# Weight splits of a two-block network move from GpSimd to VectorE, and five modulation blocks into the input projection

## The chip, the cores and the metric

The kernel runs on one core of one Trainium2 chip. The metric is the device time of one execution in microseconds. The engines of the core are named TensorE (PE in the rows), VectorE (DVE), ScalarE (ACT), GpSimd (POOL) and SyncE (SP), which issues most of the transfers. Each of them works through its own instructions in the order in which they were written or scheduled.

## The reference, cut to what matters

Two blocks run one after the other on 256 tokens of width 1024, all in float32. The first has two layers, each with a mixer and a routed network over 16384 experts; the vectors that modulate it come from one small product of the condition with `ada_w`, in twelve blocks of 512 columns per layer. The second has two layers of gated network, hybrid mixer, gated network.

```python
sh1, sc1, g1, sh2, sc2, g2 = jnp.split(cond @ ada_w[layer] + ada_b[layer], 6, axis=-1)
h = modulate(rmsnorm(x, norm1_g[layer]), sh1, sc1)
...
    y, yc = even_mixer(h, hc, ...)   # layer 0: p = h @ w_in, short convolution, gated delta rule,
                                     # neighbourhood attention, output projection
    y, yc = odd_mixer(h, hc, ...)    # layer 1: latent attention
x = x + g1[:, None, :] * y
x = x + g2[:, None, :] * peer_ffn(modulate(rmsnorm(x, norm2_g[layer]), sh2, sc2), ...)

# second block, for each of its two layers
h = swiglu(rms_norm(x, ffn1_pre[l]), ffn1_w_gate_up[l], ffn1_w_down[l])
x = x + 0.5 * rms_norm(h, ffn1_post[l])
h = hybrid_mixer(rms_norm(x, mix_pre[l]), w_in[l], ...)
x = x + rms_norm(h, mix_post[l])
h = swiglu(rms_norm(x, ffn2_pre[l]), ffn2_w_gate_up[l], ffn2_w_down[l])
x = x + 0.5 * rms_norm(h, ffn2_post[l])
```

## The kernel before

**Products in three passes.** Nearly all large products run on TensorE as three matmuls (`mm3`, L311 to L314): high part by high part, high by low, low by high. A weight slab is loaded raw by `load` (L330, 1 MB, on SyncE's queue). `hl_part` (L338) then makes the two parts of a piece of 128x1024: ScalarE casts the high part (`wh`, L343), and another engine subtracts it from the raw weight to get the low part (`wl`, written through the helper `tt`, L317). This subtraction is called a split below. The argument `e` of `hl_part` names its engine, and VectorE is the default. `feed` (L354) hands out pieces with a lookahead of two; `Slab` (L375) makes all pieces of a slab at once. In `Slab`, `e="half"` and `late=True` both give the first piece to GpSimd.

**Where GpSimd splits.** There are 84 of them: 12 for the six weight slabs of the convolution (`w_gd`, in `even_mixer`); 20 in the first layer's route stage (two at its start, the other 18 in the generator `ahead`, which makes expert weights in advance) and 22 in the second layer's (four at its start, 18 in `ahead`); and 30 at the entries of the second block's networks and mixers: five at each of four gated networks (`up_tokens`: two slabs of two pieces and the first piece of a third slab) and five at each of two hybrid mixers.

**The stages, with their times in the profiled execution.** 56 to 232 us is the input projection of the first layer in `even_mixer`: a loop of twelve convolution tiles (to about 150 us), each with one `tensor_scalar` and four `scalar_tensor_tensor` of 128x512 on VectorE; eight tiles for the attention; and the products for v and z. From 232 to 520 us, the attention stage (phase `A2`) runs several generators in turn: the inverses and the chain of the gated delta rule, the neighbourhood attention, and `ada_thread`. From 640 to 960 and from 2060 to 2300 us are the route stages: `router` picks the experts (a chain of small maximum searches on VectorE), `gbuild` builds masks out of fp16 products of 128x1024 on VectorE, and `u_ahead` runs the pieces of `ahead` through TensorE. From 2870 us on is the second block, with entries (called borders) near 2891, 3085, 3305, 3503, 3702 and 3923 us.

**The modulation blocks.** `ada_thread` (L468) makes a block of 512 columns as a sum over k: a memset of the accumulator on GpSimd, eight slices of the weight, and for each two `scalar_tensor_tensor` of 128x512 on VectorE (L326); behind that a few small matmuls. Blocks 4 to 9 of the first layer run so in the attention stage; blocks 0 to 3 are made earlier, on TensorE.

**A border of the second block.** `edge_rows` (L1942) squares the tiles of the finished product on ScalarE, takes `newton` (L405; a reciprocal root in eleven one-element steps on VectorE) of the sums, adds the scaled tile to the row store (L326, 128x512), and transposes the new rows on TensorE (L436). It does so for the two halves of 128 tokens in turn, with a second `newton` for the norm ahead of the next product. `Rows.finish` spreads the norms over a tile by one small matmul (L309). `up_tokens` and `pairs_by_token` start the next product while this goes on.

## Time and profile before

| what | value |
|---|---|
| median of 3 runs | 4130.0 us (4127.25 to 4146.29) |
| time of the profiled execution | 4132.58 us |
| its span, first to last instruction | 4130.8 us |
| TensorE busy | 3926.5 us (95%), mean granted clock 0.979 |
| VectorE busy | 2971.3 us (72%) |
| ScalarE busy | 1912.1 us (46%) |
| GpSimd busy | 752.8 us (18%) |
| moved by DMA | 862.66 MB, mean 209 GB/s |

The busy time of an engine is a mean over all stages. The granted clock is a share of full speed, and a matmul's end is modelled, so a busy TensorE is not one at its peak.

### The profile page before, as it was taken

To read this page: it belongs to the slowest core of one execution; us is meant where nothing else is said; L and a number is where in the kernel's file an instruction comes from. 1 tells how busy PE (TensorE), PEld (TensorE's weight loads), DVE (VectorE), ACT (ScalarE), POOL (GpSimd) and SP (SyncE) were. 2 spreads that over 40 slices of the span, in tenths; PEclk is the share of its full clock that TensorE was granted. 3 is DMA by queue.
4 is the path that set the end of the run, shared out by engine and by line. 5 is a ranking of instruction groups with operands and counts; after the bars stand their busy time and mean duration, and the time that the engine had idled before them with its cause. 6 is when DMAs were issued, how large, how long until landed. Compare 5 with 4: busy or idle time off the path is not lost.

```text
span 4130.8 us, 63830 instructions
## 1 busy us (share of the span) xinstructions
PE 3926.5 (95%) x24927; PEld 3537.2 (86%) x24927; DVE 2971.3 (72%) x5618; ACT 1912.1 (46%) x3241; POOL 752.8 (18%) x579
## 2 busy tenths in 40 slices
PE   8999999997999999999989999999999999999999
PEld 5877878897888787888789988888989988989988
DVE  4468579986998988847599555656668765668765
ACT  3334344772333332335558544544445454545454
POOL 2133302113444555400132000000000000000000
PEclk9999999999999999999999999999999999999999
DMA  4222133668999999843247866665454545444543
GB/s 170 92 85 79 36 148 112 221 257 309 357 362 367 369 373 362 329 173 114 87 159 279 296 227 228 229 225 202 178 187 174 184 173 180 178 179 174 184 173 143
DMA packets 234974, 862.66 MB, mean 209 GB/s; under 512 B 18944, under 2 KB 116096, under 8 KB 164528
## 3 DMA queue, kind: packets, MB, share of 16 engines
q1 hardware_dynamic: 197808, 724.35, 48.9%
q0 software_dynamic: 36864, 134.23, 8.5%
q8 instruction: 195, 3.19, 0.3%
q14 instruction: 107, 0.88, 0.1%
HBM read 795.97 MB, written 62.55 MB: 208 GB/s over the span
## 4 chain that ended last, share of the span: by engine, by line
PE 56%; DVE 15%; DMA 5%; issue 4%; POOL 2%; ACT 1%; SPq 0%; DVEq 0%; POOLq 0%; ACTq 0%
PE p L312 18%; PE p L314 18%; PE p L313 18%; DVE t L317 5%; DVE t L326 3%; DMA t<-in_pvr,c 3%; DVE wl L317 2%; POOL t L1443 2%; PE p L309 2%; DMA w<-in_pv 1%; PE p L436 1%; DVE t L1448 1%; DMA t<-in_pur,c 0%; DVE t L321 0%; ACT wh L343 0%
## 5 line engine op out<-in xcount | busy, mean ns | idle before, releaser
L317 DVE TENSOR_TENSOR wl<-w,wh 128x1024 fp32r<-128x1024 f32 (+1 forms) x933 | 1131.2, 1218 | 695.6 <-ACT wh L343 673.1
L343 ACT CAST wh<-w 128x1024 fp32r<-128x1024 f32 x1017 | 1058.8, 1048 | 986.9 <-PE p L314 435.7
L312 PE MATMUL p<-t,wh 128*128 128x256 f32 (+2 forms) x4784 | 1456.6, 305 | 20.0 <-ACT wh L343 5.3
L314 PE MATMUL p<-t,wl 128*128 128x256 f32 (+2 forms) x4784 | 1442.3, 302 | 5.3 <-DVE wl L317 3.3
L313 PE MATMUL p<-t,wh 128*128 128x256 f32 (+2 forms) x4784 | 1439.6, 301 | 1.4 <-DVE t L317 1.4
L312 PEld LDWEIGHTS p<-t,wh 128*128 128x128 f32 x4784 | 912.3, 191 | 40.8 <-ACT wh L343 7.2
L314 PEld LDWEIGHTS p<-t,wl 128*128 128x128 f32 x4784 | 912.3, 191 | 19.0 <-DVE wl L317 4.8
L313 PEld LDWEIGHTS p<-t,wh 128*128 128x128 f32 x4784 | 912.8, 191 | 17.0 <-DVE t L317 1.7
L312 PE MATMUL p<-wh,t 128*128 128x512 f32 (+3 forms) x2134 | 816.4, 383 | 27.0 <-ACT t L402 12.7
L313 PE MATMUL p<-wl,t 128*128 128x512 f32 (+3 forms) x2134 | 815.9, 382 | 22.0 <-DVE wl L317 20.8
L314 PE MATMUL p<-wh,t 128*128 128x512 f32 (+3 forms) x2134 | 813.4, 382 | 6.6 <-DVE t L317 4.6
L317 POOL TENSOR_TENSOR wl<-w,wh 128x1024 fp32r<-128x1024 f32 x84 | 225.4, 2693 | 1967.7 <-ACT wh L343 1697.7
L312 PEld LDWEIGHTS p<-wh,t 128*128 128x128 f32 x2134 | 408.3, 191 | 105.0 <-ACT t L402 14.8
L313 PEld LDWEIGHTS p<-wl,t 128*128 128x128 f32 x2134 | 408.3, 191 | 97.2 <-DVE wl L317 27.1
L314 PEld LDWEIGHTS p<-wh,t 128*128 128x128 f32 x2134 | 406.5, 191 | 87.3 <-DVE t L317 8.7
L317 DVE TENSOR_TENSOR t<-t,t 128x256 f32<-128x256 f32 (+10 forms) x732 | 352.3, 486 | 64.0 <-ACT t L402 41.5
L326 DVE SCALAR_TENSOR_TENSOR t<-t,c,t 128x512 f32<-128x512 f32 (+2 forms) x367 | 327.7, 918 | 39.6 <-DMA t<-in_pvr,c 21.1
L402 ACT CAST t<-t 128x256 fp32r<-128x256 f32 (+3 forms) x314 | 138.7, 446 | 353.3 <-DVE t L317 353.3
L309 PE MATMUL p<-t,t 128*128 128x128 f32 (+3 forms) x1536 | 225.8, 301 | 2.2 <-DVE t L326 1.9
L1443 POOL DMA_INDIRECT t<-in_pvr,c x128 | 197.5, 1543 | 155.7 <-DVE t L326 127.5
L1443 POOL DMA_INDIRECT t<-in_pur,c x128 | 171.9, 1343 | 240.5 <-DVE c L1448 198.9
L309 PEld LDWEIGHTS p<-t,t 128*128 128x128 f32 (+1 forms) x1536 | 192.9, 192 | 25.5 <-issue 11.3
(200 smaller groups left out, 3000.2 us busy)
## 6 DMA issues: line engine op xcount, KB each, us to landing
w<-in_pu SPq DMA_DIRECT2D x128, 1024.0 KB
w<-in_pv SPq DMA_DIRECT2D x128, 1024.0 KB
w<-in_fgu SPq DMA_DIRECT2D x88, 1024.0 KB
w<-in_hin SPq DMA_DIRECT2D x48, 1024.0 KB
w<-in_fdn SPq DMA_DIRECT2D x44, 1024.0 KB
gd<-t SPq DMA_DIRECT2D x20, 2048.0 KB
t<-in_ada_w SPq DMA_DIRECT2D x56, 512.0 KB
t<-gd SPq DMA_DIRECT2D x32, 768.0 KB
```

Source lines behind the costliest of these rows:

```text
L309: nc.tensor.matmul(o, l, r, start=first, stop=last)
L312: nc.tensor.matmul(o, l[0], r[0], start=first, stop=False)
L313: nc.tensor.matmul(o, l[0], r[1], start=False, stop=False)
L314: nc.tensor.matmul(o, l[1], r[0], start=False, stop=last)
L317: return (e or nc.vector).tensor_tensor(o, a, b, op)
L326: nc.vector.scalar_tensor_tensor(o, a, s, b, op0=op0, op1=op1)
L343: i = nc.scalar.copy(hi[:, :m], raw[:, s : s + m])
L402: nc.scalar.copy(dst[0], src)
L436: nc.tensor.transpose(o, i, ident[:n, :n])
L1443: nc.gpsimd.indirect_dma_start(r, None, src, at)
L1448: nc.vector.tensor_tensor_reduce(r, r, xr, 1.0, 0.0, ALU.mult, ALU.add, act[:, s : s + 1])
```

## The change

The `e` arguments that name GpSimd are taken away at the route stages' starts, in `ahead`, and at the entries of the second block, and so is the rule for first pieces in `Slab`: these 72 splits run on VectorE, and the 12 of `w_gd` stay on GpSimd. Of the six modulation blocks of the attention stage, five (4 to 8) are made in the input projection: a step of the generator `ad` behind each of the last four convolution tiles, each attention tile, and every second tile of v and z. Their weights come in 512 KB tiles (`AW`, two buffers) and two accumulators take turns. Block 9 stays behind. The scheduler may place the instructions elsewhere than the source has them.

```diff
--- before.py
+++ after.py
@@ -377,7 +377,7 @@
             raw = load(src, n)
             self.gran = gran
             self.parts = [
-                hl_part(raw, s, min(gran, n - s), nc.gpsimd if s == 0 and (late or e == "half") else None if e == "half" else e, late)
+                hl_part(raw, s, min(gran, n - s), e, late)
                 for s in range(0, n, gran)
             ]
 
@@ -684,6 +684,15 @@
         kn = vk = None
         qk = T("T16", [P, 8, 512])
         gz = pdr.tile([P, 4, 512], F32, tag="gz", name="gz")
+
+        def raws(l, n):
+            for q in range(4):
+                w = T("AW", [P, 1024])
+                nc.sync.dma_start(w, A["ada_w"][l, 2 * n + q // 2, :, q % 2 * 1024 : (q % 2 + 1) * 1024])
+                for k in range(2):
+                    yield w[:, k * 512 : (k + 1) * 512]
+
+        ad = ada_thread([(0, n, 0) for n in range(4, 9)], "AD", "G2", raws)
         with W1():
             srcs = [(A["w_gr"], 1024, None)]
             srcs += [(A["w_gd"][s], 2048, nc.gpsimd) for s in range(6)]
@@ -754,12 +763,15 @@
                 if j > 0:
                     for _ in range(3):
                         next(gstep, None)
+                if j > 7:
+                    next(ad, None)
             knT = T("T8", [P, 4, 512])
             for j in range(8):
                 W = get()
                 ps = PS("ab"[j % 2])
                 stat_tile(ps, W, 0, hT)
                 flush()
+                next(ad, None)
                 if j < 4:
                     nc.scalar.activation(qk[:, j, :], ps, AF.Copy, scale=0.125)
                 else:
@@ -791,6 +803,8 @@
                     for t in range(4):
                         for k in range(2):
                             mm3(pss[t], hT[:, 2 * q + k, HS(t)], W(k * 512, 512), q == 0 and k == 0, q == 3 and k == 1)
+                        if t % 2:
+                            next(ad, None)
                 for t in range(4):
                     if n == 0:
                         nc.vector.tensor_copy(vt[:, t, :], pss[t])
@@ -799,6 +813,8 @@
                         nc.scalar.activation(zt, pss[t], AF.Silu)
                         tt(h4(zt), h4(zt), gdv[:, None, 16:144].to_broadcast([P, 4, P]), ALU.mult, nc.gpsimd)
                         nc.sync.dma_start(gz[:, t, :], zt)
+            for _ in ad:
+                pass
 
         units = {}
         ready = set()
@@ -1093,20 +1109,14 @@
             for gn in gens:
                 yield from gn
 
-        with phase("A2", AD=2, T8=1, U=1, T4=3, S0=2, S1=2, G2=10):
+        with phase("A2", AD=1, AW=2, T8=1, U=1, T4=3, S0=2, S1=2, G2=10):
             yN = T("T8", [P, 4, 512])
             for t in (egc, kdc, bnd):
                 nc.scalar.activation(F(t), F(t), AF.Exp)
 
-            def raws(l, n):
-                for kh in range(2):
-                    w = load(A["ada_w"][l, 2 * n + kh])
-                    for k in range(4):
-                        yield w[:, k * 512 : (k + 1) * 512]
-
-            ab = [(0, n, 0) for n in range(4, 10)]
             i0, i1 = then(inv_thread(0), inv_thread(2)), then(inv_thread(1), inv_thread(3))
-            na, ad, ch = na_thread(), ada_thread(ab, "AD", "G2", raws), chain_thread()
+            na, ch = na_thread(), chain_thread()
+            ad = ada_thread([(0, 9, 0)], "AD", "G2", raws)
             hd = head_thread()
             live = [i0, ch, i1, na, na, ad, hd]
             while live:
@@ -1173,7 +1183,7 @@
             prev = (j, qy)
 
         if nt == 4:
-            Ws = [Slab(A["pq"][l, s], e="half") for s in range(2)]
+            Ws = [Slab(A["pq"][l, s]) for s in range(2)]
             pss = [PS("a") for _ in range(4)]
             for c in range(2):
                 cs = slice(256 * c, 256 * c + 256)
@@ -1320,7 +1330,7 @@
                 for e in range(4):
                     if e % 2 == 0:
                         raw = load(A["pu"][l, 2 * c + e // 2])
-                    nxt = hl_part(raw, e % 2 * 1024, 1024, nc.gpsimd if k < 2 or e == 1 else None)
+                    nxt = hl_part(raw, e % 2 * 1024, 1024)
                     if part is not None:
                         yield part
                     part = (nxt, k, e)
@@ -1519,7 +1529,7 @@
 
         @contextmanager
         def inner():
-            with phase("A1", G2=8):
+            with phase("A1", G2=8, AD=2, AW=2):
                 yield
             W1.__exit__(None, None, None)
 
@@ -1994,7 +2004,7 @@
     def pairs_by_token(srcs, hT, rows=None, then=None):
         if rows is not None:
             rows.need(0)
-        Ws = [Slab(src, e=nc.gpsimd) for src in srcs]
+        Ws = [Slab(src) for src in srcs]
         z = {}
         pss = []
 
@@ -2048,7 +2058,7 @@
 
         def up_tokens(slabs):
             rows.need(0)
-            Ws = [Slab(A["fgu"][w, s], e=nc.gpsimd) for s in slabs]
+            Ws = [Slab(A["fgu"][w, s]) for s in slabs]
             at = {}
             pss = []
```

Names below such as `wl_28720` or `t_28647` are tiles; their numbers differ between the two kernels. Lines from L700 on are 10 to 16 higher in the changed kernel.

VectorE at the border at 3085 us: the first `newton`, from its fourth step on, and the sum (128x512) behind it. Before:

```order
L317 TENSOR_TENSOR t_28624<-t_28622,t_28623 128x1
L326 SCALAR_TENSOR_TENSOR t_28624<-t_28624,t_28623 128x1
L326 SCALAR_TENSOR_TENSOR t_28623<-t_28624,t_28623 128x1
L317 TENSOR_TENSOR t_28624<-t_28622,t_28623 128x1
L317 TENSOR_TENSOR t_28624<-t_28624,t_28623 128x1
L326 SCALAR_TENSOR_TENSOR t_28624<-t_28624 128x1
L326 SCALAR_TENSOR_TENSOR t_28623<-t_28624,t_28623 128x1
L326 SCALAR_TENSOR_TENSOR t_9001<-t_28614,t_28623,t_9001 128x512
```

In the changed kernel:

```order
L317 TENSOR_TENSOR t_28648<-t_28646,t_28647 128x1
L326 SCALAR_TENSOR_TENSOR t_28648<-t_28648,t_28647 128x1
L326 SCALAR_TENSOR_TENSOR t_28647<-t_28648,t_28647 128x1
L317 TENSOR_TENSOR wl_28720<-w_28713,wh_28719 128x1024
L317 TENSOR_TENSOR t_28648<-t_28646,t_28647 128x1
L317 TENSOR_TENSOR t_28648<-t_28648,t_28647 128x1
L317 TENSOR_TENSOR wl_28726<-w_28723,wh_28725 128x1024
L326 SCALAR_TENSOR_TENSOR t_28648<-t_28648 128x1
L326 SCALAR_TENSOR_TENSOR t_28647<-t_28648,t_28647 128x1
L317 TENSOR_TENSOR wl_28730<-w_28723,wh_28729 128x1024
L326 SCALAR_TENSOR_TENSOR t_9025<-t_28638,t_28647,t_9025 128x512
```

Three splits stand between the steps of the same chain; before, no split stood there on VectorE.

VectorE in the convolution: `t_496` and `t_548` are convolution tiles, `c_332` to `c_334` belong to a small polynomial for the gates. Before:

```order
L317 TENSOR_TENSOR c_333<-c_333,c_332 128x32
L321 TENSOR_SCALAR c_333<-c_333 128x32
L326 SCALAR_TENSOR_TENSOR c_333<-c_333,c_331 128x32
L326 SCALAR_TENSOR_TENSOR c_334<-c_329,c_333 128x32
L317 TENSOR_TENSOR c_334<-c_334,c_341 128x4x4 x2
L321 TENSOR_SCALAR t_496<-t_492,c_323 128x512
L326 SCALAR_TENSOR_TENSOR t_496<-t_492,c_323,t_496 128x512 x4
L321 TENSOR_SCALAR t_548<-t_544,c_323 128x512
L326 SCALAR_TENSOR_TENSOR t_548<-t_544,c_323,t_548 128x512 x4
```

In the changed kernel, `t_902` and `t_1168` are accumulators of modulation blocks:

```order
L326 SCALAR_TENSOR_TENSOR t_902<-t_1067,c_78,t_902 128x512
L326 SCALAR_TENSOR_TENSOR t_496<-t_492,c_323,t_496 128x512
L323 TENSOR_SCALAR c_333<-c_332 128x32
L326 SCALAR_TENSOR_TENSOR t_902<-t_1067,c_78,t_902 128x512
L326 SCALAR_TENSOR_TENSOR t_496<-t_492,c_323,t_496 128x512
L317 TENSOR_TENSOR c_333<-c_333,c_332 128x32
L326 SCALAR_TENSOR_TENSOR t_1168<-t_1172,c_78,t_1168 128x512
L326 SCALAR_TENSOR_TENSOR t_496<-t_492,c_323,t_496 128x512
L321 TENSOR_SCALAR t_548<-t_544,c_323 128x512
L321 TENSOR_SCALAR c_333<-c_333 128x32
L326 SCALAR_TENSOR_TENSOR t_1168<-t_1172,c_78,t_1168 128x512
L326 SCALAR_TENSOR_TENSOR t_548<-t_544,c_323,t_548 128x512
```

Convolution steps and accumulations take turns, and the gates' steps, which all stood ahead of this tile, lie between them. In the whole projection 80 accumulations are new: 10 ahead of the first convolution tile's gates (L703), 22 to the last convolution tile, 48 behind it.

VectorE in the second route stage, where `router`'s searches of a token block end and `gbuild`'s products (`t_...<-c,c`) begin. Before:

```order
L1217 MAX t_19148<-t_19150 128x8
L1214 MAX t_19148<-t_19143 128x8
L317 TENSOR_TENSOR wl_19228<-w_19225,wh_19227 128x1024
L326 SCALAR_TENSOR_TENSOR c_17728<-p_19008,c_17726 128x128
L317 TENSOR_TENSOR t_19050<-c_17722,c_17724 128x1024
L317 TENSOR_TENSOR t_19050<-c_17722,c_17725 128x1024
L317 TENSOR_TENSOR t_19050<-t_19050,c_17726 128x1024
L317 TENSOR_TENSOR t_19116<-c_17722,c_17724 128x1024
L317 TENSOR_TENSOR t_19116<-c_17722,c_17725 128x1024
L317 TENSOR_TENSOR t_19116<-t_19116,c_17726 128x1024
L317 TENSOR_TENSOR t_19116<-t_19116,c_17727 128x1024
```

In the changed kernel:

```order
L1226 MAX_INDEX t_19173<-t_19172,t_19167 128x8
L1227 MAX t_19172<-t_19174 128x8
L317 TENSOR_TENSOR wl_19186<-w_19106,wh_19185 128x1024
L1228 MAX_INDEX t_19173<-t_19172,t_19174 128x8
L317 TENSOR_TENSOR t_19217<-c_17746,c_17748 128x1024
L317 TENSOR_TENSOR t_19217<-c_17746,c_17749 128x1024
L317 TENSOR_TENSOR t_19217<-t_19217,c_17750 128x1024
L317 TENSOR_TENSOR wl_19252<-w_19249,wh_19251 128x1024
L317 TENSOR_TENSOR t_19283<-c_17746,c_17748 128x1024
L317 TENSOR_TENSOR t_19283<-c_17746,c_17749 128x1024
L317 TENSOR_TENSOR t_19283<-t_19283,c_17750 128x1024
```

Two splits of weight pieces for `u_ahead` stand between the searches and products here, where one stood.

## Rows read from the trace of the kernel before

**Rows 1.** the page's costliest groups: count | busy us, mean ns | idle before.

```profile
L317 DVE TENSOR_TENSOR wl<-w,wh 128x1024 fp32r<-128x1024 f32 (+1 forms) x933 | 1131.2, 1218 | 695.6 <-ACT wh L343 673.1
...
L317 POOL TENSOR_TENSOR wl<-w,wh 128x1024 fp32r<-128x1024 f32 x84 | 225.4, 2693 | 1967.7 <-ACT wh L343 1697.7
```

**Rows 2.** stages: busy us (instructions) by engine, granted clock, DMA share, GB/s.

```profile
56.00:150.00 94.00, 91.27 (x443) 74.66 (x442) 61.58 (x106) 33.26 (x54) 27.27 (x33) 0.96 0.20 73
150.00:232.00 82.00, 82.00 (x362) 66.27 (x362) 25.39 (x27) 22.02 (x28) 0.00 (x0) 1.00 0.28 103
232.00:520.00 288.00, 262.10 (x1842) 225.69 (x1841) 205.78 (x411) 123.96 (x299) 110.41 (x92) 0.95 0.20 69
640.00:960.00 320.00, 302.57 (x2170) 287.59 (x2169) 282.50 (x858) 203.59 (x431) 62.80 (x28) 0.98 0.58 206
2060.00:2300.00 240.00, 222.31 (x2047) 217.97 (x2046) 215.51 (x618) 163.82 (x347) 64.16 (x22) 0.98 0.63 225
```

**Rows 3.** timeline of VectorE, border at 3085: start, us, operation, idle before.

```profile
3076.59 2.13 DVE L317 TENSOR_TENSOR t<-t,t 128x256 fp32r<-128x256 f32 x1 [0.47 <-ACT t L402]
...
3084.34 0.35 DVE L326 SCALAR_TENSOR_TENSOR t<-t,t 128x1 f32<-128x1 f32 x2
3084.72 4.60 DVE L317 TENSOR_TENSOR t<-t,t 128x1 f32<-128x1 f32 x2
3089.36 2.26 DVE L326 SCALAR_TENSOR_TENSOR t<-t 128x1 f32<-128x1 f32 x1
3091.65 0.16 DVE L326 SCALAR_TENSOR_TENSOR t<-t,t 128x1 f32<-128x1 f32 x1
```

**Rows 4.** timeline of GpSimd, same border.

```profile
3084.59 7.01 POOL L317 TENSOR_TENSOR wl<-w,wh 128x1024 fp32r<-128x1024 f32 x3 [6.14 <-ACT wh L343]
```

**Rows 5.** timeline of TensorE, same border.

```profile
3092.66 1.75 PE L436 MATMUL p<-c,t 128*128 128x128 f32 x7 [5.15 <-DVE t L326]
```

**Rows 6.** waits of TensorE, 2870 to 4130: total us, times, longest.

```profile
PE p L436 <- DVE t L326: 25.4, 5, 5.2
PE p L309 <- DVE t L326: 5.6, 5, 1.7
PE p L436 <- DVE t L317: 4.8, 1, 4.8
```

**Rows 7.** timeline of ScalarE, border at 3085.

```profile
3086.18 1.06 ACT L343 CAST wh<-w 128x1024 fp32r<-128x1024 f32 x1 [0.30 <-PE p L314]
```

**Rows 8.** timeline of TensorE, border at 3305.

```profile
3313.26 1.12 PE L436 MATMUL p<-c,t 128*128 128x128 f32 x4 [4.92 <-DVE t L326]
```

**Rows 9.** busy us by engine and granted clock behind the wait at 3092.

```profile
3090.00:3098.00 8.00, 5.34 (x25) 5.14 (x26) 7.34 (x20) 3.39 (x12) 1.85 (x7) 0.57 0.84 321
```

**Rows 10.** timeline of TensorE, border into the second route stage.

```profile
2043.61 1.11 PE L436 MATMUL p<-c,t 128*128 128x128 f32 x4 [5.93 <-DVE t L321]
```

**Rows 11.** groups of VectorE by shape, first route stage (640 to 960).

```profile
L317 DVE TENSOR_TENSOR t<-c,c 128x1024 f16<-128x1024 f16 x96 | 71.3, 779 | 1.5 <-PE p L309 1.0 <-ACT c L1270 0.5
L317 DVE TENSOR_TENSOR t<-t,c 128x1024 f16<-128x1024 f16 x72 | 47.3, 683 | 0.0
```

**Rows 12.** groups of GpSimd by shape, first route stage.

```profile
L317 POOL TENSOR_TENSOR wl<-w,wh 128x1024 fp32r<-128x1024 f32 x18 | 51.5, 2859 | 251.3 <-ACT wh L343 85.4 <-DVE t L1159 83.6 <-DVE t L317 36.4
```

**Rows 13.** groups of VectorE by shape, projection: the convolution's steps.

```profile
L326 DVE SCALAR_TENSOR_TENSOR t<-t,c,t 128x512 f32<-128x512 f32 x48 | 39.7, 827 | 2.1
```

**Rows 14.** groups of VectorE by shape, attention stage: the accumulations.

```profile
L326 DVE SCALAR_TENSOR_TENSOR t<-w,c,t 128x512 f32<-128x512 f32 x96 | 82.6, 887 | 0.6 <-DMA w<-in_ada_w 0.6
```

**Rows 15.** the accumulations: ns minimum/median/maximum, first and last start.

```profile
L326 DVE SCALAR_TENSOR_TENSOR t<-w,c,t x96: 724/742/1737, 248.5 to 426.8; 128x512 f32<-128x512 f32 x96
```

**Rows 16.** groups of TensorE by shape, attention stage: the modulation blocks' matmuls.

```profile
L309 PE MATMUL p<-c,t 128*128 128x1 f32 x64 | 7.8, 247 | 0.7 <-PE p L309 0.4 <-DVE t L326 0.3
...
L309 PE MATMUL p<-t,c 128*2 128x512 f32 x8 | 3.9, 592 | 0.0
```

**Rows 17.** waits of TensorE, 232 to 520 us.

```profile
PE p L436 <- DVE t L321: 12.2, 6, 4.6
```

## The prediction

> **What bounds the kernel now.** I first read the costliest groups. A 1 MB weight slab is cut into pieces of 128x1024; the low part of a piece (weight minus its rounded high part) costs VectorE 1218 ns and GpSimd 2693 ns, and GpSimd makes 84 of them beside VectorE's 933 [rows 1]. Seventy-two of the 84 move. Then the stages: TensorE is busy 91 to 100% of each, so only what it waits for, or what is added to its own work, moves the end. In the projection it is busy 91.3 of 94 and 82.0 of 82 us, in the attention stage behind it (232 to 520) 262 of 288; in the two route stages VectorE is busy 282.5 of 320 and 215.5 of 240 us, nearly as much as TensorE, and is a second bound there [rows 2].
>
> Last, the borders of the second block, where TensorE has used up its projection and waits for a row norm. What to see is the chain of one-element steps (`newton`) that VectorE runs there. Two steps in a row normally take 0.35 us together; but the two that began at 3084.72 took 4.60 us, the next 2.26 us, and only at 3091.65 is a step short again [rows 3]. Just in that stretch GpSimd made three splits, 7.01 us from 3084.59 on [rows 4]: a small VectorE step that starts beneath a GpSimd split ends when that split ends. TensorE stood idle for 5.15 us, till the sum behind the chain was there [rows 5]. In the whole second block it waited 25.4 us in five such places, 4.8 us in a sixth, and 5.6 us in five shorter ones for the row that ends a border [rows 6].
>
> **Borders of the second block** (30 splits: 20 for the four FFN entries, 10 for the two hybrid entries). Take the border at 3085. Now: from 3084.72 to 3091.65 the chain needs 6.93 us for three steps that cost 0.19 us each alone (0.35 for two, and the gap between starts), so 6.4 us are lost. Changed: three splits stand in VectorE's own queue inside the chain, after its sixth, eighth and tenth step, as the order of instructions shows. VectorE takes 1.22 us for each, 3.7 us. They need their high parts from ScalarE; the last of the three casts began at 3086.18 and took 1.06 us [rows 7], so it ends at 3087.24, while the third split can begin only at 3084.72 + 2 x 1.22 + 4 x 0.19 = 3087.9. No wait arises, and 6.4 - 3.7 = 2.7 us are won. A fourth split, ahead of the chain, held a 128x256 step for 2.13 us [rows 3]; with 1.22 us on VectorE instead the chain starts some 1.0 us sooner. So 3.7 us for each of the two hybrid entries: 7.4.
>
> At an FFN entry behind a hybrid mixer (3305 and 3923) TensorE waits 4.92 us [rows 8]. Into the chain come three splits and one 512-wide product that stood behind it: 6.5 lost, less 3.7 and 0.7, gives 2.1 us, twice: 4.3. At the entry behind an FFN (3503), where fewer splits are ahead of the sum, 4.0; at the first entry (2891) 2.5, as part of the wait there is for a split itself. These two are estimates by the same steps. Sum: 18.2 us. Lower bound, if the splits wait for their casts one after the other: half, 9. Upper bound: the whole 25.4 + 4.8 = 30.
>
> In the last chain of an FFN entry five splits, 6.1 us on VectorE, now stand ahead of the row that a small matmul needs. GpSimd's splits hold that chain today too, and TensorE waits there 1.7 us at the longest [rows 6]; in the new order it has some 18 more matmuls in front of that wait. I count it as nothing; without that cover it costs some 2 us at each of the four, 8 in all.
>
> **The clock.** Behind such a gap the granted clock is lower: 0.57 of full speed from 3090 to 3098 [rows 9], so a part of that stretch ran at 1.2 instead of 2.4 GHz, and 0.43 x 8 = 3.4 us were lost. Six borders: 20 us at most. The gaps get shorter, not zero, and a shorter one need not keep the clock. Between 0 and 20 I take 5, since over half of each gap stays.
>
> **The borders of the first block.** Where the second layer's route stage begins TensorE waits 5.93 us behind three GpSimd splits [rows 10]; with three splits on VectorE in its place, 3 us by the reckoning above (0 to 6). The attention-to-route border has two splits: 1.
>
> **Bodies of the route stages** (36 splits). VectorE gets 36 x 1.22 = 44 us more, where it is idle for 37.5 and 24.5 us [rows 2]. What does it get back? The fp16 products of 128x1024 with two constant inputs take 779 ns in the mean over 96 of them, their neighbours of the same shape 683 [rows 11]: this group alone loses 96 x 0.096 = 9.2 us in the first stage. A GpSimd split lasts 2.86 us there [rows 12], so 36 x 2.86 = 103 us is the most that 36 can hold. Over all steps that overlap a split, the time beyond the usual one of their kind adds up, instruction by instruction, to 20 us in the first stage and 19 in the second. I take these 39: VectorE becomes 5 us busier, and the time 4 us longer, as TensorE has 17 us of gaps in each stage. Bounds: +35 with only the 9.2 given back, -20 if VectorE's idle time takes up half of the splits.
>
> **The front** (five of six modulation blocks). 80 accumulations of 128x512, 10 MB of loads and their matmuls leave the attention stage for the projection; no work is new. VectorE is busy 61.6 of 94 us up to 150 us [rows 2]. A convolution step of this shape takes 0.83 us there [rows 13], so the 32 accumulations that the new order puts ahead of the last convolution tile add 27 us: 88 of 94, beside GpSimd's eleven splits. That is near the edge; some convolution step that a matmul needs comes late, and I put 5 us on it. The other 48 (40 us) find 57 idle us behind 150. The loads go into 176 us, 57 GB/s beside the present 73 and 103: no bound. In SP's queue the 512 KB loads stand between the weight loads, and each waits for one of two buffers, so a late accumulation holds the weight loads behind it; the projection looks two pieces ahead, and I see this as part of the 5 us.
>
> The attention stage loses 80 x 0.887 = 71 of VectorE's 206 us [rows 14].
>
> The Trainium skill (GPSIMD Engine Reference, Key points) says that GpSimd shares its memory interfaces with VectorE and that VectorE instructions with two inputs in memory contend. The trace agrees for accumulations, whose slowest took 1737 ns at a median of 742 [rows 15]. By that rule the accumulations that land beside the eleven splits pay most; it is a reason for rival 1 below.
>
> TensorE's share of the modulation blocks is 7.8 us for the 128x1 form, of which three blocks in four move, and 3.9 us for the other, which moves whole [rows 16]: 5.9 + 3.9 = 9.8. In the projection TensorE has 2.7 idle us, so +10. The attention stage loses 10 of work, and of its 26 us of gaps some: the largest item, 12.2 us in six waits for VectorE [rows 17], is partly chains of dependent steps, which stay. I take 8. Front: +10 + 5 - 10 - 8 = -3, with bounds of +15 (stalls, and nothing gained behind) and -22.
>
> **Sum.** The profiled execution took 4132.6 us (span 4130.8, 1.8 around it); the median of the runs is 4130.0. -18.2 - 5 - 4 + 4 - 3 = -26: 4106.4 from the former, 4103.8 from the latter. I say 4105.
>
> **Rivals.**
> 1. *The front stalls, or the borders pay later.* For: VectorE at 88 of 94 us with accumulations that were seen at up to 1.7 us; five splits in front of a row at FFN entries. Against: those waits have cover in TensorE's order. Front +10 instead of -3, or 8 more at the borders, or part of both: 4113 to 4120.
> 2. *The attention stage is freed.* For: a third of VectorE's work goes, in a stage whose six threads share its queue. 20 of 26 us of gaps vanish instead of 8, and the clock rises with it (0.95 there): 4089 to 4093.
> 3. *VectorE becomes the bound of the route stages: slower.* If the time lost beneath GpSimd lay in VectorE's slack, nothing comes back, and all 42 splits of the first block's route stages and their borders are added to a bound: 42 x 1.22 = 51. 4132.6 + 51 - 18 - 3 = 4163, no clock regained. It passes 4151 once less than 12 of the 39 us come back. For: VectorE is at 88 and 90% there. Against: 9.2 us of one group are read off directly.
>
> **Chances.** Forecast 0.45, rival 1 0.27, rival 2 0.20, rival 3 0.08. A change of 0.5% is 20.6 us (to 4109.4 or 4150.7), about what a measurement of this kernel can tell from none. Faster: most of the forecast (0.38), rival 2, a little of rival 1: 0.60. Slower: most of rival 3, 0.07. Same: 0.33. The range 4086 to 4127 takes in rival 2 and rival 1 with both its prices (4130 less a few) and leaves out rival 3; the forecast's own is 4097 to 4112.
>
> **What would show it.** Borders: no one-element step above 0.2 us, splits of 1.22 us between them, and TensorE's waits for L326 near 12 us instead of 25. Route stages as long as before within 5 us, with VectorE above 90%. The projection some 15 us longer, the attention stage 18 shorter. Wrong would be: waits of TensorE for low parts of tens of us in the route stages, or a projection that grows by over 25.

## The result, and the profile after

The changed kernel takes 4067.5 us in the median of four runs (4065.4 to 4075.8), the one before 4135.3 on the same chip; the ratio is 0.984, 95% interval 0.9825 to 0.9855. That is 60 to 72 us faster, where 26 were forecast, and below the range. The profiled span went from 4130.8 to 4063.6 us.

Both traces hold 24927 matmuls of TensorE. The start of the n-th in one against the n-th in the other gives the stages' share of the 67.2 us:

| stretch of before | forecast | by the traces |
|---|---|---|
| projection and attention stage (56 to 520) | -3 | -6.7 |
| attention-to-route border | -1 | -3.6 |
| first route stage (640 to 960) | +2 | -11.6 |
| gather stage (960 to 1740) | 0 | -5.6 |
| latent attention (1740 to 2025) | 0 | +1.3 |
| border into the second route stage | -3 | -3.0 |
| second route stage (2060 to 2300) | +2 | -6.7 |
| to the second block (2300 to 2870) | 0 | -1.0 |
| second block's borders, clock with them | -23 | -6.0, -6.9, -3.5, -4.3, -6.0, -3.5 |

The stages of the changed kernel: busy us by engine (TensorE, its weight loads, VectorE, ScalarE, GpSimd), granted clock, DMA share, GB/s. The first two rows are the projection to its last matmul and the attention stage, then the two route stages, then the clock at the border that stood at 3085.

```profile
56.00:254.60 198.60, 192.23 (x893) 153.30 (x893) 142.68 (x216) 58.60 (x86) 35.07 (x40) 0.98 0.36 128
254.60:513.40 258.80, 236.34 (x1756) 207.96 (x1755) 146.75 (x328) 120.53 (x294) 98.76 (x86) 0.96 0.11 36
...
630.00:938.00 308.00, 299.00 (x2169) 284.66 (x2168) 280.27 (x874) 202.73 (x430) 18.87 (x10) 0.99 0.59 214
2031.00:2264.00 233.00, 221.65 (x2045) 216.43 (x2044) 215.97 (x636) 165.57 (x347) 3.99 (x4) 0.99 0.64 232
...
3040.00:3048.00 8.00, 5.72 (x32) 4.36 (x31) 7.86 (x18) 6.58 (x18) 0.00 (x0) 1.00 0.67 255
```

Against [rows 2], VectorE is busy for nearly the same time in both route stages (282.5 and 280.3; 215.5 and 216.0 us), 36 splits more included, and the stages are 12 and 7 us shorter. Behind this border the clock stays at 1.00, where it was 0.57 [rows 9].

VectorE at that border, as in [rows 3]:

```profile
3040.10 0.35 DVE L326 SCALAR_TENSOR_TENSOR t<-t,t 128x1 f32<-128x1 f32 x2
3040.37 1.22 DVE L317 TENSOR_TENSOR wl<-w,wh 128x1024 fp32r<-128x1024 f32 x1
3041.50 0.34 DVE L317 TENSOR_TENSOR t<-t,t 128x1 f32<-128x1 f32 x2
3041.77 1.23 DVE L317 TENSOR_TENSOR wl<-w,wh 128x1024 fp32r<-128x1024 f32 x1
3042.91 0.15 DVE L326 SCALAR_TENSOR_TENSOR t<-t 128x1 f32<-128x1 f32 x1
3043.10 0.16 DVE L326 SCALAR_TENSOR_TENSOR t<-t,t 128x1 f32<-128x1 f32 x1
3043.18 1.22 DVE L317 TENSOR_TENSOR wl<-w,wh 128x1024 fp32r<-128x1024 f32 x1
```

Three splits of 1.22 us stand among steps that are all short; no row waits for a cast. TensorE there (against [rows 5]), and then its waits in the second block (against [rows 6]):

```profile
3045.11 1.32 PE L436 MATMUL p<-c,t 128*128 128x128 f32 x8 [1.84 <-DVE t L326]
```

```profile
PE p L436 <- DVE t L326: 9.7, 5, 2.1
PE p L314 <- DVE t L326: 3.8, 10, 0.6
PE p L309 <- DVE t L326: 2.9, 3, 1.0
PE p L309 <- DVE t L317: 2.4, 1, 2.4
```

The five long waits have shrunk from 25.4 to 9.7 us, none of them above 2.1.

### The profile page after: what moved, and what is told of

It is laid out like the page before. It is cut to its first block, busy times and chain, and to the rows that moved or that the text cites. A ratio compares the mean times of both kernels' runs of the same rounds, so it can differ in the third digit from the quotient of the medians.

```text
span 4063.6 us, 63754 instructions
## 1 busy us (share of the span) xinstructions
PE 3911.3 (96%) x24927; PEld 3520.6 (87%) x24927; DVE 2936.7 (72%) x5690; ACT 1913.4 (47%) x3241; POOL 563.5 (14%) x507
## 4 chain that ended last, share of the span: by engine, by line
PE 67%; DVE 16%; DMA 6%; issue 5%; ACT 2%; POOL 2%; SPq 0%; DVEq 0%; POOLq 0%; ACTq 0%
PE p L312 20%; PE p L314 20%; PE p L313 20%; PE p L309 6%; DVE t L317 5%; DVE t L326 4%; DVE wl L317 4%; DMA t<-in_pvr,c 3%; DMA w<-in_pv 2%; PE p L436 2%; POOL t L1453 1%; DVE t L1458 1%; DMA t<-in_pur,c 1%; ACT wh L343 1%; DVE t L321 0%
## 5 line engine op out<-in xcount | busy, mean ns | idle before, releaser
L317 DVE TENSOR_TENSOR wl<-w,wh 128x1024 fp32r<-128x1024 f32 (+1 forms) x1005 | 1217.3, 1216 | 672.1 <-ACT wh L343 650.1
L312 PE MATMUL p<-t,wh 128*128 128x256 f32 (+2 forms) x4784 | 1452.7, 304 | 17.6 <-ACT wh L343 4.9
L313 PE MATMUL p<-wl,t 128*128 128x512 f32 (+3 forms) x2134 | 812.6, 381 | 17.4 <-DVE wl L317 17.4
L326 DVE SCALAR_TENSOR_TENSOR t<-t,c,t 128x512 f32<-128x512 f32 (+2 forms) x463 | 398.5, 892 | 43.1 <-DMA t<-in_pvr,c 20.2
L317 DVE TENSOR_TENSOR t<-t,t 128x256 f32<-128x256 f32 (+10 forms) x732 | 319.9, 442 | 62.3 <-ACT t L402 37.9
L309 PE MATMUL p<-t,t 128*128 128x128 f32 (+3 forms) x1536 | 217.5, 297 | 1.2 <-POOL t L317 1.0
L309 PEld LDWEIGHTS p<-t,t 128*128 128x128 f32 (+1 forms) x1536 | 187.5, 188 | 21.7 <-issue 8.3
L1458 DVE CUSTOM_DVE_ANT_0 t<-t,t 128x1024 f32<-128x1024 f32 x128 | 153.0, 1216 | 11.2 <-DMA t<-in_pur,c 11.2
```

Source lines behind the costliest of these rows:

```text
L309: nc.tensor.matmul(o, l, r, start=first, stop=last)
L312: nc.tensor.matmul(o, l[0], r[0], start=first, stop=False)
L313: nc.tensor.matmul(o, l[0], r[1], start=False, stop=False)
L317: return (e or nc.vector).tensor_tensor(o, a, b, op)
L326: nc.vector.scalar_tensor_tensor(o, a, s, b, op0=op0, op1=op1)
L1458: nc.vector.tensor_tensor_reduce(r, r, xr, 1.0, 0.0, ALU.mult, ALU.add, act[:, s : s + 1])
```

## The experiments

Fifteen runs were made, one of them of the changed kernel once more. Differences in us below are the ratio of the runs times 4135, with its interval; what is said of a stage comes from the trace of a single execution. A VectorE step that starts beneath a GpSimd instruction and is kept until that instruction ends is called held, and the lost time a hold.

**One part of the change alone.** The first three kernels are the one before with one part.

```diff
 # route stages only
-            Ws = [Slab(A["pq"][l, s], e="half") for s in range(2)]
+            Ws = [Slab(A["pq"][l, s]) for s in range(2)]
-                    nxt = hl_part(raw, e % 2 * 1024, 1024, nc.gpsimd if k < 2 or e == 1 else None)
+                    nxt = hl_part(raw, e % 2 * 1024, 1024)
-        Ws = [Slab(src, e=nc.gpsimd) for src in srcs]
+        Ws = [Slab(src, e=nc.gpsimd if rows is not None else None) for src in srcs]
```

> Only the 42 splits of the two route stages and their starts move to VectorE; the second block and the front stay as before. By the stages of the changed kernel's trace these hold 25 us of its gain (attention-to-route border 3.6, first route stage 11.6, second border 3, second stage 6.7). Theory L (a VectorE step that starts beneath a GpSimd split is held, and TensorE waits for that step): 20 to 28 us faster than before. The prediction's own term (VectorE near its bound, 5 us busier): within 3 us of no gain. If the changed kernel's gain there came from the earlier start that the front gave it: under 10.

Measured: ratio 0.9928 (0.9915 to 0.9942), 24 to 35 us faster. The route stages and their borders gain by themselves; the front is not needed.

```diff
 # second block's borders only
-                hl_part(raw, s, min(gran, n - s), nc.gpsimd if s == 0 and (late or e == "half") else None if e == "half" else e, late)
+                hl_part(raw, s, min(gran, n - s), nc.gpsimd if s == 0 and e == "half" else None if e == "half" else e, late)
-        Ws = [Slab(src, e=nc.gpsimd) for src in srcs]
+        Ws = [Slab(src, e=nc.gpsimd if rows is None else None) for src in srcs]
-            Ws = [Slab(A["fgu"][w, s], e=nc.gpsimd) for s in slabs]
+            Ws = [Slab(A["fgu"][w, s]) for s in slabs]
```

> Only the 30 splits at the six borders of the second block move. Theory L with the held chain as the prediction reckoned it: 23 us faster (18 of waits, 5 of clock). By the changed kernel's stages: 30 us. If the borders need the changed order of the front or the route stages: clearly less than 18.

Measured: 0.9916 (0.9903 to 0.9928), 30 to 40 us faster, and by the trace -5.0, -6.9, -3.5, -4.4, -6.0 and -3.5 at the six borders, as in the changed kernel.

The third has the change's lines on `raws`, `ad` and the two phases, and none on splits.

> Only the five modulation blocks move; all 84 splits of GpSimd stay. The prediction's term: 3 us faster (between 15 slower and 22 faster). By the changed kernel's stages: 7 us faster. If moving the blocks also frees the stage border behind the attention stage: about 10.

Measured: 0.9973 (0.9962 to 0.9984), 7 to 16 us faster. The three add up to 76 us against the whole's 66; the four intervals together allow for the difference.

**Idle splits: is the hold a cause in the route stages?** The changed kernel with GpSimd work that nothing depends on. The order on TensorE, VectorE, ScalarE and in the load queue is unchanged.

```diff
                     nxt = hl_part(raw, e % 2 * 1024, 1024)
+                    if k < 2 or e == 1:
+                        tt(const_idle, f(nxt[0][:, :1024]), f(nxt[0][:, :1024]), ALU.subtract, nc.gpsimd)
```

> The changed kernel, with 36 further subtractions of 128x1024 on GpSimd in the route stages, one for each split that moved there; nobody reads what they write. Theory L (the lock itself costs): the 18 us of the two stages are lost again, 46 to 50 us faster than before instead of 64 to 67. Rival D (TensorE waited for the low parts that GpSimd delivered late): nothing is lost, 64 to 67.

Measured: 0.9899 (0.9884 to 0.9913), 36 to 48 us faster; 24 of the 66 are lost, more than the 18 that theory L expected. The two stages:

```profile
630.00:953.00 323.00, 303.56 (x2170) 288.12 (x2169) 298.70 (x874) 203.37 (x431) 89.23 (x29) 0.98 0.58 206
2047.00:2294.00 247.00, 226.39 (x2043) 220.75 (x2042) 231.11 (x635) 165.14 (x347) 97.44 (x22) 0.96 0.60 219
```

VectorE runs the same instructions and is busy 18 and 15 us longer; the stages are 15 and 14 us longer. TensorE waits for none of this work, so rival D, late low parts, cannot explain the loss; nor does a wait for a low part of GpSimd stand among TensorE's waits of either route stage in the kernel before. The hold costs.

**The splits of the bodies left out.**

```diff
-                    nxt = hl_part(raw, e % 2 * 1024, 1024)
+                    nxt = hl_part(raw, e % 2 * 1024, 1024, low=not (k < 2 or e == 1))   # returns (hi, hi)
```

> The changed kernel, with the 36 splits of the route stages' bodies left out: those pieces use their high part in place of the low one, so the output differs there. VectorE has 44 us less to do in the two stages. If VectorE bounds them, as the prediction assumed when it turned busy time into stage time: at least 25 us faster than the changed kernel, 90 or more faster than before. If TensorE bounds them and the change only took away waits for single held steps: at most 10 us faster than the changed kernel, 66 to 76 faster than before.

Measured: 0.9828 (0.9807 to 0.9849), 62 to 80 us faster; 3 to 5 us better than the changed kernel in the mean, within the intervals; the 25 that a bound of VectorE would have given are out. The two stages:

```profile
629.50:937.00 307.50, 299.79 (x2170) 285.74 (x2169) 262.57 (x858) 203.51 (x431) 11.76 (x10) 0.99 0.59 215
2027.00:2253.50 226.50, 218.31 (x2047) 214.86 (x2048) 198.33 (x618) 164.07 (x348) 7.01 (x4) 0.99 0.67 239
```

The order of instructions matters for what this shows. The change also re-ordered the route stages: compared line by line, without tile numbers, TensorE's order in the changed kernel differs from the one before in 278 lines in the first stage and 1654 in the second (of 2168 and 2045 matmuls, a moved one counted twice). The kernel without these splits has TensorE's order of the kernel before again (0 and 28 lines; VectorE 90 and 12, ScalarE 300 and 30). So against the kernel before it tells what GpSimd's 36 splits cost where they stood: 12.5 and 13.7 us. The changed kernel wins 11.6 and 6.7 of these 26; 44 us of VectorE's work and the new order together cost it the other 8, and no run tells those two apart.

**Quartered splits.** The kernel before, each GpSimd split in four instructions; the order on TensorE, VectorE and ScalarE is unchanged.

```diff
-        i = tt(lo[:, :m], raw[:, s : s + m], f(hi[:, :m]), ALU.subtract, e)
+        g = m if e is None else 256
+        for c in range(0, m, g):
+            i = tt(lo[:, c : c + g], raw[:, s + c : s + c + g], f(hi[:, c : c + g]), ALU.subtract, e)
```

> The kernel before, each of GpSimd's 84 splits cut into four of 128x256, on GpSimd as before. Theory L1 (a VectorE step that starts beneath a GpSimd instruction is held until that instruction ends, and one gets through between two): the chains at the borders take 0.6 us for a step instead of 2.3, the borders win 3 to 4 us each, the route stages about half of their 18: 25 to 35 us faster than before. Theory L2 (VectorE is shut out as long as GpSimd has work queued, or slowed in proportion to GpSimd's busy time): within 5 us of before.

Measured: 0.9919 (0.9901 to 0.9938), 26 to 41 us faster, and by the trace nearly all of it in the second block (29 of 34). At the border at 3085, VectorE and then GpSimd:

```profile
3076.77 1.31 DVE L317 TENSOR_TENSOR t<-t,t 128x1 f32<-128x1 f32 x2
3078.11 0.67 DVE L326 SCALAR_TENSOR_TENSOR t<-t 128x1 f32<-128x1 f32 x1
3078.81 0.67 DVE L326 SCALAR_TENSOR_TENSOR t<-t,t 128x1 f32<-128x1 f32 x1
```

```profile
3076.63 9.27 POOL L317 TENSOR_TENSOR wl<-w,wh 128x256 fp32r<-128x256 f32 x12 [3.87 <-ACT wh L343]
```

Twelve pieces of 0.77 us, and each step of the chain takes 0.67: it is held until the GpSimd instruction ends, and one gets through between two. The rest of the chain, four steps, is done within four pieces. Theory L1 holds for chains. The route stages gained 0.7 and 3.6 us only, against the half of 18 that was expected: VectorE's queue is nearly full there, and its fp16 products with two constant inputs still took 0.73 us in the mean (0.78 before, 0.69 in the changed kernel).

**Idle copies.** Three GpSimd copies, one input each, in place of each idle subtraction.

```diff
-                        tt(const_idle, f(nxt[0][:, :1024]), f(nxt[0][:, :1024]), ALU.subtract, nc.gpsimd)
+                        [nc.gpsimd.tensor_copy(const_idle, f(nxt[0][:, :1024])) for _ in range(3)]
```

> The changed kernel with three GpSimd copies of 128x1024 (one input each) for each of the 36 splits of the route stages, read by nobody: about as much GpSimd time as the idle subtractions, which cost 24 us. If any busy GpSimd instruction holds VectorE: 15 to 24 us are lost again, 42 to 50 faster than before. If the hold comes from two-input work on GpSimd alone: under 5 lost, 60 to 66 faster than before.

Measured: 0.9941 (0.9921 to 0.9960), 17 to 33 us faster; 42 are lost, more than with subtractions and more than either expectation had. The copies in the first stage:

```profile
L1336 POOL COPY t<-wh 128x1024 f32<-128x1024 f32 x54 | 113.7, 2105 | 240.5 <-ACT wh L343 149.7 <-DVE t L1169 88.4
```

One input is enough for a hold: beside the copies VectorE's 58 splits took 1.34 us in the mean, without them 1.21. GpSimd is busy 114 us instead of the subtractions' 77 (18 of 4.27 us in the mean), but these sums are no measure of the holds, as they contain GpSimd's own waiting. Of the 36 idle subtractions 30 took 1.9 to 2.9 us and six 7.7 to 27. GpSimd in the first stage of the idle splits:

```profile
883.62 29.59 POOL L317 TENSOR_TENSOR t<-wh 128x1024 f32<-128x1024 f32 x2 [20.16 <-ACT wh L343]
```

The first of these two took 27.1 us. VectorE ran its products one behind the other all that time at their usual length; the step after its first gap was held for 1.86 us:

```profile
908.65 0.30 DVE L317 TENSOR_TENSOR t<-t 128x128 f32<-128x128 f16 x1
908.99 1.86 DVE L326 SCALAR_TENSOR_TENSOR t<-t 128x128 int32<-128x128 f32 x1
```

**Early or late splits.** The kernel before, with only a part of the bodies' splits moved; the first line of + is the early kernel, the second the late one.

```diff
-                    nxt = hl_part(raw, e % 2 * 1024, 1024, nc.gpsimd if k < 2 or e == 1 else None)
+                    nxt = hl_part(raw, e % 2 * 1024, 1024, nc.gpsimd if k >= 2 and e == 1 else None)
+                    nxt = hl_part(raw, e % 2 * 1024, 1024, nc.gpsimd if k < 2 else None)
```

> The kernel before, with only the first eight GpSimd splits of each route stage's body on VectorE (16 in all; most run while the router's searches do and before the mask products begin). Theory P (a held step costs only where TensorE waits for the mask products; of the 20 us that VectorE loses in the first stage 17 lie there): 0 to 4 us faster. Rival, every split gives the same: 16 of 36 of the 18 us, 8 faster.

Measured: 1.0077 (1.0062 to 1.0092), 26 to 38 us slower: both expectations fell. In the first route stage TensorE now waited for one of GpSimd's remaining splits, which it did not before:

```profile
PE p L314 <- POOL wl L317: 7.2, 1, 7.2
```

The two stages were 20.7 and 17.6 us longer, so this wait is only a part. The order of instructions on TensorE and VectorE had changed with it (276 and 458 lines of difference in the first stage), so this run says nothing on single holds; it does say that a split left on GpSimd can itself be waited for, and that an order can cost as much as the change gave in these stages.

> The kernel before, with only the other ten GpSimd splits of each route stage's body on VectorE (20 in all; they run among the mask products). Theory P: 14 to 18 us faster, nearly all that the bodies gave. Every split the same: 10. Prediction's reading, VectorE's time spent against VectorE's time returned (24 us against some 22): within 3 us of none.

Measured: 0.9955 (0.9938 to 0.9971), 12 to 26 us faster, as theory P had it, but with an order changed in the same way. The next two keep the order: the idle subtractions again, for the early pieces alone (`if k < 2`) and for the late ones alone (`if k >= 2 and e == 1`).

> The changed kernel with idle GpSimd subtractions only for the first eight pieces of each route stage (16 in all); the order on TensorE, VectorE, ScalarE and in the load queue is that of the changed kernel. Theory P (holds cost where TensorE waits for mask products, not among the router's searches): 0 to 5 of the 24 us that 36 of them cost are lost, 60 to 66 us faster than before. Each hold alike: 16 of 36, 11 us lost, 55 faster.

Measured: 0.9853 (0.9831 to 0.9876), 51 to 70 us faster: about 7 lost of the 68 that the changed kernel gave when run again (below).

> The same for the other ten pieces only (20 in all). Theory P: 18 to 24 us lost, 42 to 48 faster than before. Each hold alike: 13 lost, 53 faster.

Measured: 0.9880 (0.9858 to 0.9902), 41 to 59 us faster: about 19 lost. By the traces the stages grew by 4.2 and 5.5 us with 16 early subtractions (0.6 us each), by 9.3 and 9.3 with 20 late ones (0.9 each). The means point theory P's way, but early ones are not free, and the two intervals overlap. A reason for a difference is in the trace of the kernel before. GpSimd, and VectorE beneath it:

```profile
667.35 2.39 POOL L317 TENSOR_TENSOR wl<-w,wh 128x1024 fp32r<-128x1024 f32 x1 [7.58 <-ACT wh L343]
```

```profile
667.40 0.28 DVE L1162 MAX8 t<-t 128x8 f32<-128x128 f32 x1
667.59 0.28 DVE L1159 MAX8 t<-t 128x8 f32<-128x128 f32 x1
668.11 0.28 DVE L1160 MATCH_REPLACE8 t<-t,t 128x128 f32<-128x128 f32 x1
```

The router's searches are not held at all: 154 of them began beneath a GpSimd split in the two stages, and none took longer than 0.30 us, which is the longest elsewhere too.

> The changed kernel with the 36 idle subtractions on VectorE instead of GpSimd, 22 us more in its own queue in each route stage; the order of the other queues shifts in places. If VectorE's time in all decides: as much as the idle GpSimd splits cost, 20 to 30 us lost, 36 to 46 faster than before; the prediction's reading would give 44 lost. If only the held single steps matter: under 8 lost, 58 or more faster.

Measured: 0.9902 (0.9882 to 0.9922), 32 to 49 us faster: about 28 lost for 44 us of added VectorE work, 0.64 us for each. The two stages:

```profile
629.80:948.30 318.50, 303.74 (x2170) 285.62 (x2169) 300.05 (x893) 205.57 (x431) 16.67 (x9) 0.98 0.58 209
2044.30:2298.10 253.80, 228.85 (x2046) 221.06 (x2046) 236.20 (x654) 165.48 (x347) 3.92 (x4) 0.96 0.59 213
```

So VectorE's own time does seem to count near this load, at less than its full price. But TensorE's order differs from the changed kernel's here too (482 and 606 lines in the two stages), so the 28 us are not the price of the work alone.

**Two larger versions, and the changed kernel again.**

```diff
 # attention stage: five products and sums of 128x512, for example
-                tt(h4(kg), h4(kn[:, t, :]), bc4(egc[:, t, d, :]), ALU.mult, nc.gpsimd)
+                tt(h4(kg), h4(kn[:, t, :]), bc4(egc[:, t, d, :]), ALU.mult)
 # the convolution's splits
-            srcs += [(A["w_gd"][s], 2048, nc.gpsimd) for s in range(6)]
+            srcs += [(A["w_gd"][s], 2048, None) for s in range(6)]
```

> The changed kernel with the 76 products and sums of 128x512 that GpSimd makes in the attention stage moved to VectorE too (52 us more of VectorE in a stage where it is idle for 129 of 277 us). Theory L: VectorE's held steps there get short, TensorE waits less for the chain; 5 to 12 us faster than the changed kernel, 70 to 78 faster than before. Rival: in this stage the products are themselves links of dependent chains that run side by side on the two engines, and one engine makes them later: 0 to 15 us slower than the changed kernel.

Measured: 0.9833 (0.9812 to 0.9853), 61 to 78 us faster: not to be told from the changed kernel. Neither theory L's 5 to 12 us nor a clear loss came.

> The changed kernel with the last twelve GpSimd splits (the convolution's weights) on VectorE as well. VectorE loses 18 us there by held steps and gets 14.6 us of splits: busy about as now, 85 to 89 of 102 us. TensorE waits only 6.4 us in the whole projection, so at most some 5 us to win: 0 to 5 faster than the changed kernel, 64 to 72 faster than before. Rival, VectorE late for the convolution's weights, since accumulations and splits share one queue: 3 to 12 slower than the changed kernel.

Measured: 0.9835 (0.9820 to 0.9851), 62 to 74 us faster.

> The changed kernel itself on the chip of these runs, as the measure for the one with all splits on VectorE: 64 to 68 us faster than before, and the gather stage (938 to 1712 us of its first trace) 3 to 8 us shorter than before if that part of the gain is real, 0 if it was one execution's chance.

Measured: 0.9835 (0.9818 to 0.9851), 62 to 75 us faster, on the same chip as the one before; the two cannot be told apart. In the projection the first row is the changed kernel, the second the one with all splits on VectorE:

```profile
L326 DVE SCALAR_TENSOR_TENSOR t<-t,c,t 128x512 f32<-128x512 f32 x127 | 95.7, 791 | 3.3 <-DMA t<-in_ada_w 2.2
```

```profile
L326 DVE SCALAR_TENSOR_TENSOR t<-t,c,t 128x512 f32<-128x512 f32 x128 | 89.7, 744 | 0.2
```

The steps go back to their length alone, 0.74 us, and the time does not change, as TensorE waits for hardly any of them. The gather stage of this second execution was 0.9 us shorter than before, not 5.6, and between 0.5 and 10.5 shorter in the other traces whatever their edit: that row of the first table is chance of single executions, the one of the kernel before among them.

## Why the prediction was wrong

**The step that failed** is the price of the route stages' bodies: "I take these 39: VectorE becomes 5 us busier, and the time 4 us longer". Its first half was nearly right. The fp16 products went back to their length, and VectorE's busy time stayed as it was, within 2.3 us. All instructions but the splits are 39 us shorter in sum over the two stages, just what the prediction had. In the first stage (against [rows 11]):

```profile
L317 DVE TENSOR_TENSOR wl<-w,wh 128x1024 fp32r<-128x1024 f32 x56 | 67.9, 1214 | 21.0 <-ACT wh L343 16.8 <-PE p L309 4.2
L317 DVE TENSOR_TENSOR t<-c,c 128x1024 f16<-128x1024 f16 x96 | 62.8, 687 | 2.0 <-ACT c L1280 2.0
```

The second half, from a balance of busy time to stage time, was wrong: the stages became 18 us shorter at equal busy time. It gave a held microsecond and a worked one the same price. The runs give two: these holds, 39 us of VectorE's time, cost the stages 26 (the kernel without these splits against the one before), and 44 us of VectorE's work with the new order cost 8. VectorE's idle time fell from 37.5 to 27.7 and from 24.5 to 17.0 us, TensorE's from 17.4 to 9.0 and from 17.7 to 11.4, and the clock rose from 0.98 to 0.99. TensorE's waits in the first stage, before and after:

```profile
PE p L309 <- DVE t L317: 9.8, 8, 2.8
PE p L436 <- DVE t L1214: 5.3, 1, 5.3
```

```profile
PE p L436 <- DVE t L317: 7.1, 3, 5.1
PE p L309 <- DVE t L317: 1.1, 3, 0.4
```

The eight waits for `gbuild`'s products, 9.8 us, are down to three of 1.1 us in all. Two things stand behind the bad price, as far as the rows go. The first is place. The stretch from the first to the last mask product, where VectorE is idle for only 8.8 and 7.7 us:

```profile
696.70:922.30 225.60, 208.74 (x1627) 199.10 (x1628) 216.79 (x511) 163.30 (x376) 34.86 (x14) 0.97 0.62 224
2139.10:2280.30 141.20, 130.71 (x1268) 127.69 (x1269) 133.50 (x251) 110.70 (x259) 37.87 (x10) 0.97 0.73 263
```

and in the changed kernel:

```profile
689.90:901.60 211.70, 203.15 (x1614) 193.95 (x1615) 208.05 (x520) 162.80 (x375) 13.63 (x5) 0.98 0.65 237
2111.90:2244.30 132.40, 125.63 (x1235) 121.64 (x1234) 130.66 (x257) 112.63 (x259) 1.38 (x2) 0.97 0.73 266
```

VectorE has 8.7 and 2.8 us less to do there: of the 36 new splits only 15 fall into these stretches, 20 among the router's searches ahead of them, while 26 of the 39 us that the holds had taken came back here (durations of all instructions but the splits, summed in both traces). The second is mutual waiting. VectorE's idle time in these two stretches (length less busy) fell from 8.8 to 3.7 and from 7.7 to 1.7 us, TensorE's from 16.9 to 8.6 and 10.5 to 6.8. That a held step lets TensorE wait, and that TensorE's delay then comes back to VectorE, is my reading of these rows; the runs show that holds cost the stages 29 us for 34 us by which VectorE is busy longer (idle splits), and VectorE's own work 31 us for 40 (idle subtractions on VectorE, the changed order included), not how the waits pass between the engines. That the second stage gained 6.7 us with nearly the same work on VectorE is not explained further.

The gain of 18 us lies within the bound of -20 that the prediction gave this term, and the borders within theirs of 30; the range was drawn from the rivals and took in neither. Both bounds together would have come to about 4071.

**The borders of the second block**: right mechanism, undersized. The waits named in the trace fell from 45.1 to 20.7 us in all (all rows of both answers, the shorter ones not shown), 24.4 instead of 18.2; the rest of the 30.2, 5.8 us, is the clock and small gaps, where 5 were taken. In the order of the borders the waits fell by 3.9, 4.6, 2.8, 5.3, 5.0 and 2.8 us, where 2.5, 3.7, 2.1, 4.0, 3.7 and 2.1 were taken: each term was too small, by 0.7 to 1.4. At the first entry TensorE had also waited 2.8 us for GpSimd's own low parts. The 3.4 us of clock reckoned at 3085 count a stretch in which TensorE stood idle up to 3092.66 [rows 5]; beside the waits 2.3 us were won there. The cover ahead of the small matmul held: the waits of L309 came to 5.3 us, as before.

**The front**: -6.7 instead of -3, with the parts as reckoned: the projection from its start to its last matmul is 14.5 us longer (forecast 15), the attention stage 22.1 shorter (18). **The first block's borders** gave 6.6 instead of 4.

**The rivals.** The slower case (VectorE as the bound, 51 us added) may have had a core: 44 us of VectorE work that bring nothing back cost 28, in another order. But what was held came back in full. The stall of the front did not come. The freed attention stage came in a small part.

The Trainium skill (GPSIMD Engine Reference, Key points) gives contention for VectorE instructions in a two-port mode or with two inputs in memory. The 128x512 steps of the projection agree (0.79 us beside GpSimd's splits, 0.74 without), and so do the maximum searches, with one input, which were not held. The full 128x1024 splits on VectorE, with two inputs as well, took 1.22 us in the mean before, but only because few met a GpSimd split: 5 of 82 in the two route stages began beneath one, and two of these took 1.45 and 2.26 us. Beside the idle subtractions 11 of 118 took 1.3 to 2.9 us, in the changed kernel none. The `tensor_scalar` steps of 128x512, with one input, were held too (five of five that began beneath a split in the projection before, 1.57 us in the mean instead of 0.48); in which mode they ran no row shows.

## What to carry to other kernels

Before giving GpSimd some of VectorE's work, look at VectorE's smallest steps beneath it in the trace: where a step of 0.16 us shows the length of the other engine's instruction, a split moved to VectorE costs 1.22 us and gives back up to 2.3 in such a chain; among the products and searches of the route stages it gave back 1.1 of VectorE's time. If the work has to stay there, cut it into short instructions; a chain of small steps then passes between them, as the quartered splits show. Where two in-order engines are both near their bound, do not price a change by the sum of busy time over the stage: take the stretch in which they wait for each other, and count their idle time as a part of what can be won. Compare the order of instructions before two runs are set against each other, as an edit of one argument can re-order a whole stage.

## What was not expected of the hardware

A one-element step of the chain that starts beneath a GpSimd split takes until that split ends, whatever its own length: 2.26 us beneath splits of 2.34, 0.67 beneath pieces of 0.77. A longer step still has its own work to do then: four fp16 products of 128x1024 in the first route stage ended 0.55 us behind the split that held them and took 2.88 us instead of 0.68. It needs no second input on GpSimd's side: copies hold too. Not every step is held, as the searches show. And GpSimd can be the one that waits: behind an unbroken run of VectorE's products one idle subtraction took 27.1 us, where those among the searches took mostly 1.89.
